# A layer with attention, retention and a gated MLP: the hand-written order at the start of the up projection ends earlier, and GpSimd's sums for the third column unit are tied there

## The chip, the cores and the metric

The kernel runs on one core of one Trainium2 chip. The metric is device time in microseconds (us) of one execution. TensorE (PE) multiplies, VectorE (DVE), ScalarE (ACT) and GpSimd (POOL) do the elementwise work, and SyncE (SP) issues most of the DMAs. Each engine runs its own list of instructions in order and waits where an instruction needs something that another engine or a DMA has not yet delivered.

## The reference

One layer of a diffusion backbone over 1024 latent tokens of width 1024, in fp32. An attention and a retention branch are merged and added to `x`; the change lies behind all that, where the MLP begins:

```python
hx2 = _modulate(_rmsnorm(x, norm2_g[l]), sh2, sc2)
x = x + g2 * _conv_ffn(hx2, w_up[l], conv_w[l], conv_b[l], w_down[l])
...
def _conv_ffn(h, w_up, conv_w, conv_b, w_down):
    u = h @ w_up                                   # (1024 x 1024) @ (1024 x 5632)
    n = u.shape[1]
    pad = CONV_W // 2
    up = jnp.pad(u, ((0, 0), (pad, pad), (0, 0)))
    u = sum(up[:, i:i + n] * conv_w[i] for i in range(CONV_W)) + conv_b
    a, val = jnp.split(u, 2, axis=-1)
    return (jax.nn.silu(a) * val) @ w_down
```

`D_FF` is 2816, so `u` has 5632 columns; `CONV_W` is 3 and runs along the tokens.

## The kernel before, in words

**Precision.** A product of fp32 matrices is made of three passes over operands that are split in a high and a low part (`split`, L86 and L87): ScalarE casts the block to fp32r (the high half), and VectorE subtracts that from the block (the low half). `open3` issues high x high, high x low and low x high as `PE L1374`. A weight tile is `wc` in the profile; the raw blocks that it is split from are `ur` (loaded), `s` (summed) or `raw`.

**The up projection.** The columns of `w_up` are worked off in units: a unit holds one block of gate columns and the block of value columns that goes with it, and computes `u` for both and all tokens, as a 2 x 2 product by seven multiplications in place of eight. The weight's quarters are a11, a12, a21, a22, and four sums of them s1 to s4; the moving side has the quarters B11, B21, B22 and four differences of quarters, the "combinations" T1 to T4. The seven products are a11·B11, s2·T2, s1·T1, s3·T3, a12·B21, a22·T4 and s4·B22, each of twelve 128x512 matmuls. The class `Seven` holds the general form: `load` reads the four raw quarters and makes s1 to s4 on GpSimd (L1388 to L1391), `prod` splits a weight and multiplies, `step` says what belongs to each product. The banks are named X, Y, Z and W; sums of banks on VectorE (`p1`, `u2`, `u3`, in tiles `pu`) give the four quarters of `u` (tiles `uu`), and `conv` (L1815 to L1840) makes the convolution and the gate of a finished unit.

**The start by hand.** The last token block, `LAST` (block 7 of 8), is still being normalized when the up projection begins. Two units, n = 0 and 1 (`EARLY` is 2), therefore begin early: their weight sums stand ready in memory (`us`, from `d_u`), and each product of theirs is issued as soon as the part of the moving side that it needs is there. The order of this stretch is written out by hand in a block `with tc.manual_schedule():` (L1924 to L2006). Within it, every engine gets its instructions in the order of the code. Outside of it a scheduler sets each engine's order at build time. The functions of the stretch:

- `copy_p1(n)` copies the first product of unit n out of its bank on ScalarE (L1796), so that a12·B21 may be added into the same bank.
- `norm_rows(LAST, g)` writes the normalized rows of the last block, on ScalarE (L1714, `h2h`, and L1716, `vr`) and VectorE; `norm_comb` (L1725) makes the last block's part of a combination. Its results stand in `vo` and `vr`.
- `comb_raw(c, b)` loads block b of combination c+1 from the scratch `d_t` (tile `tr`, on SP's queue, L1781). `comb_split(c, b, t)` splits it into the tiles of T1 to T4. Blocks 0 to 2 come from the scratch, block 3 is the last token block's.
- `close(0)`, `close(1)` and `close(2)` of a unit make its products with T2, T3 and T4 and VectorE's sums with them. In `close(0)` of before, the parameters `first` and `last` cut the work of unit 1 in two: `first=False` issues the product alone, `last=False` the sums alone.
- `units[2].load(with_vec)` loads the quarters of unit 2, the first that is not early. `with_vec` ties the first of its four GpSimd sums to the last VectorE instruction written before it:

```python
def with_vec(ins):
    prev = next(i for i in reversed(nc.cur_bb.bb.instructions) if i.engine == mybir.EngineType.DVE)
    tc.add_manual_dep(ins.ins, prev.name, mybir.DependencyInfo(mybir.DependencyClass.Sync, mybir.DependencyReason.DATA))
```

In before that instruction is the convolution's L1824 of unit 0, since `units[0].close(2)`, which completes unit 0, is the last line of the block. Behind the block the loop over `interleaved(EARLY, NF)` makes the steps of all further units, in the scheduler's order.

Of the kernel before, what the change touches and what calls it, by code (L numbers as in the profile page):

```python
# [8 lines left out]
F32 = mybir.dt.float32  # L9
# [7 lines left out]
P = 128  # L17
# [15 lines left out]
NF = FF // P  # L33
# [7 lines left out]
def tile_hybrid_layer(ctx, tc: tile.TileContext, io, dbg=None):  # L41
    nc = tc.nc
    vec, act, pool, pe, sync = nc.vector, nc.scalar, nc.gpsimd, nc.tensor, nc.sync
# [265 lines left out]
    first = [[wtile() for _ in range(2)] for _ in range(3)]  # L309
# [702 lines left out]
    us = []  # L1012
# [274 lines left out]
    mix, last = None, (None, None)  # L1287
    for h in range(RH):
        head = Head(h)
        for i in range(NCB + NTB):  # L1290
# [3 lines left out]
            last = (head, i)  # L1294
# [336 lines left out]
    EARLY = 2  # L1631
# [132 lines left out]
    def w_split(raw):  # L1764
        w = wtile()
        split(w[:, 0], w[:, 1], raw)
        return w
# [11 lines left out]
    def comb_raw(c, b):  # L1779
        t = gtile(0, F32, "tr")  # L1780
        sync.dma_start(t, d_t[c, b])  # L1781
        return t

    def comb_split(c, b, t):
        split(combs[f"T{c + 1}"][0][:, b], combs[f"T{c + 1}"][1][:, b], t if len(t.shape) == 3 else t.rearrange("p (k t) -> p k t", k=KH))
# [8 lines left out]
    def copy_p1(n):  # L1794
        p1e.append(gtile(0, F32, "pu"))
        act.copy(p1e[n], early[n][0][:, 0:512])  # L1796
# [48 lines left out]
    class Up(Seven):  # L1845
# [19 lines left out]
            self.p1, self.W = p1e[self.n], early[self.n][1][:, 512:1024]  # L1865
            self.c11()

        def close(self, n, first=True, last=True):
            if n == 0:
                if first and last or not first:  # L1870
                    self.u2, self.u3 = (self.tmp() for _ in range(2))
                    self.prod(self.Y, us[self.n, 1], "T2", True, False)
                if not first:
                    return
                vec.tensor_tensor(self.u2, self.Y, self.p1, ALU.add)
                vec.tensor_tensor(self.u2, self.W, self.u2, ALU.add)
                self.add(0, 1, self.Z, self.u2)
            elif n == 1:
                self.prod(self.Y, us[self.n, 2], "T3", False, False)
                vec.tensor_tensor(self.u3, self.Y, self.p1, ALU.add)  # L1880
                self.add(1, 1, self.Z, self.u3)
            else:
                self.prod(self.Y, a22[self.n], "T4", False, True)
                self.add(1, 0, self.Y, self.p1)
# [31 lines left out]
    with tc.manual_schedule():  # L1916
        out_begin(LAST)
        ra = [up_raw(n, 0, 0) for n in range(EARLY)]
        norm_begin(LAST - 1)
        norm_begin(LAST)  # L1920
        out_mm(LAST, 0)
        wu[0, "a11"], wu[1, "a11"] = w_split(ra[0]), w_split(ra[1])
        out_add(LAST, 0)
        out_mm(LAST, 1, range(0, KH))  # L1924
        norm_turn(LAST - 1, 1)
        norm_turn(LAST - 1, 0)
        out_mm(LAST, 1, range(KH, KB))
        ra = [up_raw(n, 0, 1) for n in range(EARLY)]
        tr = {(0, b): comb_raw(0, b) for b in range(2)}
        norm_rows(LAST - 1, 1)  # L1930
        norm_rows(LAST - 1, 0)
        early.append(early_bank(0))
        mm_seven(early[0][0][:, 0:512], wu[0, "a11"], h2_rows(0, 0), True, False)
        out_add(LAST, 1)
        norm_square(LAST)
        po.release()
        pu.append(ps("u_ps1", "left"))
        wop.release()
        gpool[1].release()
        rp = sb("raws", "right")  # L1940
        tpl = sb("combs", "right")
        us = {(n, 3): ur_load(d_u[n, 3]) for n in range(EARLY)}
        for c in ("T1", "T2", "T3", "T4"):
            combs[c] = [tpl.tile([P, 4, KH, P], F32R, name=f"{c}{i}") for i in range(2)]
        sync.dma_start(d_x1[LAST * P : NTB * P], tok[LAST]["x"])
        cs = {c: norm_comb(LAST - 1, c) for c in (0, 2)}
        norm_scale(LAST)
        cs.update({c: norm_comb(LAST - 1, c) for c in (1, 3)})
        wu[0, "a12"] = w_split(ra[0])
        wu[1, "a12"] = w_split(ra[1])  # L1950
        early.append(early_bank(1))
        mm_seven(early[1][0][:, 0:512], wu[1, "a11"], h2_rows(0, 0), True, False)
        norm_turn(LAST, 1, early[0][1][:, 0:512])
        norm_turn(LAST, 0, early[1][1][:, 0:512])
        copy_p1(0)
        for c in range(4):
            store_comb(LAST - 1, c, cs[c])
        us.update({(n, c): ur_load(d_u[n, c]) for c in (0, 1, 2) for n in range(EARLY)})
        a22 = [ur_load(units[n].src[1, 1]) for n in range(EARLY)]
        op.release()  # L1960
        tap = sb("conv", "right")
        mm_seven(early[0][0][:, 0:512], wu[0, "a12"], h2_rows(KH, 0), False, True)
        wu[0, "s4"] = w_split(us[0, 3])
        norm_rows(LAST, 1)
        copy_p1(1)
        mm_seven(early[1][0][:, 0:512], wu[1, "a12"], h2_rows(KH, 0), False, True)
        norm_rows(LAST, 0)
        tr[0, 2] = comb_raw(0, 2)
        mm_seven(early[0][1][:, 512:1024], wu[0, "s4"], h2_rows(KH, 1), True, True)
        wu[1, "s4"] = w_split(us[1, 3])  # L1970
        mm_seven(early[1][1][:, 512:1024], wu[1, "s4"], h2_rows(KH, 1), True, True)
        for b in range(2):
            comb_split(0, b, tr[0, b])
        t0 = norm_comb(LAST, 0)
        wu[0, "s1"] = w_split(us[0, 0])
        comb_split(0, 2, tr[0, 2])
        comb_split(0, 3, t0)
        mm_seven(early[0][1][:, 0:512], wu[0, "s1"], comb_rows("T1"), True, True)
        tr.update({(c, b): comb_raw(c, b) for c in (1, 2) for b in range(3)})
        wu[1, "s1"] = w_split(us[1, 0])  # L1980
        t2 = norm_comb(LAST, 2)
        t1 = norm_comb(LAST, 1)
        mm_seven(early[1][1][:, 0:512], wu[1, "s1"], comb_rows("T1"), True, True)
        units[0].open()
        units[1].open()
        comb_split(1, 3, t1)
        for b in range(3):
            comb_split(1, b, tr[1, b])
        t3 = norm_comb(LAST, 3)
        units[0].close(0)  # L1990
        units[1].close(0, first=False)
        comb_split(2, 3, t2)
        for b in range(3):
            comb_split(2, b, tr[2, b])
        units[1].close(0, last=False)
        units[0].close(1)
        tr.update({(3, b): comb_raw(3, b) for b in range(3)})
        cw = tap.tile([P, 2 * NF, 3], F32, name="cw")
        sync.dma_start(cw, io["conv_w"])
        cb = tap.tile([P, 2 * NF], F32, name="cb")  # L2000
        sync.dma_start(cb, io["conv_b"])
        comb_split(3, 3, t3)
        for b in range(3):
            comb_split(3, b, tr[3, b])
        units[1].close(1)
        units[0].close(2)  # L2006
    units[2].load(with_vec)
    units[2].step(0)
    units[1].close(2)
    for i, n in interleaved(EARLY, NF):  # L2010
# [239 lines left out]
```

## Time and profile before

| | |
|---|---|
| time, median of 3 runs | 1794.78 us (1793.72 to 1796.03) |
| the profiled execution | 1792.47 us, of which the span of its instructions 1790.7 |
| TensorE busy | 1724.9 us, 96%, 8333 matmuls |
| VectorE busy | 1322.9 us, 74% |
| ScalarE busy | 853.9 us, 48% |
| GpSimd busy | 585.0 us, 33% |
| DMA | 265.28 MB, mean 148 GB/s |
| granted TensorE clock, mean | 0.985 |

Busy shares are averages over the whole span. Of the forty equal slices of the span (44.8 us each), TensorE is at nine tenths or more in all but five; two of the five, with seven and six tenths, are the slices from 1119 to 1209 us, and the granted clock there is eight tenths. The hand-written stretch at the start of the up projection lies there.

### The profile page before, as it was taken

Reading aid. Unit: us, or ns where it says so; the run is one execution under the profiler, and the core shown is the slowest. Engines: PE = TensorE matmul, PEld = TensorE weight load, DVE = VectorE, ACT = ScalarE, POOL = GpSimd, SP = SyncE. Lnnn points to the kernel's source line nnn. Section 1 sums busy time; section 2 is a strip of 40 time slices with the busy share of each in tenths; the row PEclk is TensorE's granted clock in tenths of the full one; section 3 lists DMA queues with packets and bytes.
Section 4 is the critical chain, followed back from the end, with each engine's and each line's share of the span. In section 5 each row is a group of like instructions: output and inputs, shape, how many; then the busy total and the mean of one; then the engine's idle time right before and its main releaser. Section 6 shows DMA issues by size and latency. Waiting matters only on the chain.

```text
span 1790.7 us, 24670 instructions
## 1 busy us (share of the span) xinstructions
PE 1724.9 (96%) x8333; PEld 1428.3 (80%) x8333; DVE 1322.9 (74%) x2444; ACT 853.9 (48%) x1843; POOL 585.0 (33%) x485
## 2 busy tenths in 40 slices
PE   7799999999999999999999999769999999999997
PEld 3588888888888888788888887658888888788886
DVE  4978888766776776866755577589889989876755
ACT  5667666553443444543443234444444444554444
POOL 2610000003334343565403221065555555211444
PEclk9899999999999999999999999889999999999999
DMA  8133334432231213577567557332332333486753
GB/s 341 56 123 120 108 115 138 130 120 96 75 103 42 72 42 118 169 247 241 178 233 268 198 200 255 118 112 88 99 108 88 103 120 101 165 285 196 236 170 147
DMA packets 142143, 265.28 MB, mean 148 GB/s; under 512 B 16160, under 2 KB 28608, under 8 KB 142016
## 3 DMA queue, kind: packets, MB, share of 16 engines
q1 hardware_dynamic: 121360, 234.86, 40.0%
q10 hardware_dynamic: 20656, 28.84, 4.4%
q8 instruction: 65, 1.06, 0.2%
q14 instruction: 62, 0.51, 0.1%
HBM read 190.49 MB, written 70.53 MB: 146 GB/s over the span
## 4 chain that ended last, share of the span: by engine, by line
PE 45%; issue 5%; DVE 4%; POOL 3%; ACT 1%; DMA 0%; POOLq 0%; DVEq 0%; ACTq 0%
PE u L1374 30%; PE y L1374 4%; PE pr L111 2%; PE pr L112 2%; PE pr L110 2%; PE om L123 2%; PE om L122 2%; PE om L121 2%; DVE wc L87 1%; POOL x L2064 1%; PE pn L112 1%; PE pn L110 1%; PE pn L111 1%; POOL pd L2101 0%; DVE at L1821 0%
## 5 line engine op out<-in xcount | busy, mean ns | idle before, releaser
L1374 PE MATMUL u<-T,wc 128*128 128x512 f32 x1056 | 256.9, 400 | 20.7 <-DVE wc L87 9.3
L1374 PEld LDWEIGHTS u<-T,wc 128*128 128x128 f32 x1056 | 201.9, 193 | 69.2 <-DVE wc L87 11.8
L1374 PE MATMUL y<-wc,ahl 128*128 128x512 f32 x924 | 212.3, 392 | 3.1 <-DVE wc L87 1.8
L1374 PEld LDWEIGHTS y<-wc,ahl 128*128 128x128 f32 x924 | 174.5, 189 | 40.5 <-DVE wc L87 2.5
L87 DVE TENSOR_TENSOR wc<-ur,wc 128x512 fp32r<-128x512 f32 x147 | 132.5, 905 | 64.3 <-ACT wc L86 64.3
L86 ACT CAST wc<-ur 128x512 fp32r<-128x512 f32 x147 | 90.9, 622 | 121.2 <-PE y L1374 72.1
L1374 PE MATMUL u<-h2a,wc 128*128 128x512 f32 x528 | 125.2, 392 | 5.7 <-DVE pu L1422 3.5
L111 PE MATMUL mm<-low,wc 128*128 128x512 f32 (+1 forms) x328 | 124.1, 378 | 0.0
L1374 PEld LDWEIGHTS u<-h2a,wc 128*128 128x128 f32 x528 | 98.9, 188 | 28.2 <-issue 3.4
L110 PE MATMUL mm<-hx,wc 128*128 128x512 f32 x264 | 107.6, 408 | 0.3 <-DVE vc L221 0.3
L112 PE MATMUL mm<-hx,wc 128*128 128x512 f32 x264 | 105.1, 398 | 0.0
L86 ACT CAST wc<-s 128x512 fp32r<-128x512 f32 x80 | 49.7, 622 | 93.8 <-PE u L1374 88.7
L1513 POOL TENSOR_TENSOR col<-col,bcol 128x32 f32<-128x32 f32 x1 | 0.2, 250 | 281.9 <-DVE aw L538 281.9
L123 PE MATMUL mm<-wc,low 128*128 128x512 f32 (+1 forms) x240 | 91.3, 381 | 0.0
L1374 PE MATMUL u<-hxT,wc 128*128 128x512 f32 x384 | 89.8, 390 | 0.0
L87 DVE TENSOR_TENSOR wc<-s,wc 128x512 fp32r<-128x512 f32 x80 | 88.3, 1105 | 0.3
L1374 PEld LDWEIGHTS u<-hxT,wc 128*128 128x128 f32 x384 | 72.0, 188 | 15.2 <-issue 0.3
L87 DVE TENSOR_TENSOR wc<-raw,wc 128x512 fp32r<-128x512 f32 x88 | 67.2, 774 | 21.1 <-ACT wc L86 20.9
L1388 POOL TENSOR_TENSOR s<-ur 128x512 f32<-128x512 f32 x20 | 33.8, 1690 | 143.6 <-DVE wc L87 68.1
L121 PE MATMUL mm<-wc,hx 128*128 128x512 f32 x192 | 75.3, 392 | 0.6 <-ACT r L1105 0.6
L122 PE MATMUL mm<-wc,hx 128*128 128x512 f32 x192 | 75.3, 392 | 0.0
L87 DVE TENSOR_TENSOR wc<-wr,wc 128x512 fp32r<-128x512 f32 x56 | 54.6, 979 | 23.1 <-ACT wc L86 22.9
(395 smaller groups left out, 4642.0 us busy)
## 6 DMA issues: line engine op xcount, KB each, us to landing
ur<-in_w_up SPq DMA_DIRECT2D x82, 256.0 KB, 2.8
ur<-d_a SPq DMA_DIRECT2D x77, 256.0 KB, 3.0
aw<-in_w_ada SPq DMA_DIRECT2D x32, 512.0 KB, 3.3
pj<-in_w_down SPq DMA_DIRECT2D x44, 256.0 KB, 4.7
d_w<-pj SPq DMA_DIRECT2D x44, 256.0 KB, 2.0
d_a<-sa SPq DMA_DIRECT2D x44, 256.0 KB, 2.0
ur<-d_w SPq DMA_DIRECT2D x44, 256.0 KB, 3.5
d_a<-at SPq DMA_DIRECT2D x33, 256.0 KB, 2.6
```

Source lines behind the costliest of these rows:

```text
L86: act.copy(hi, src)
L87: (lo_eng or vec).tensor_tensor(lo, src, hi.bitcast(F32), ALU.subtract)
L110: pe.matmul(out, wh, xh, start=k == 0, stop=False)
L111: pe.matmul(out, wh, xl, start=False, stop=False)
L112: pe.matmul(out, wl, xh, start=False, stop=k == n - 1)
L121: pe.matmul(out, ah, bh, start=first, stop=False)
L122: pe.matmul(out, ah, bl, start=False, stop=False)
L123: pe.matmul(out, al, bh, start=False, stop=last)
L1374: pe.matmul(out, a, b, start=first and n == 0, stop=last and n == 2, skip_group_check=True)
L1388: pin(pool.tensor_tensor(self.s1, self.a21, self.a22, ALU.add))
L1513: pool.tensor_tensor(col[:, 16:48], col[:, 16:48], bcol[:, 16:48], ALU.add)
L2064: pool.tensor_tensor(z, z, fg[:, gs(dh)], ALU.mult)
```

## The change

It has three parts. In the block, `copy_p1(1)` moves ahead of `norm_rows(LAST, 1)`. The block now ends behind `comb_split(2, 3, t2)`, which is the last token block's split of the third combination, T3; all that followed in it is outside, in the scheduler's hands, and `units[2].load(with_vec)` stands first there, so that the tie is to that split. The loads of T4's three blocks now stand with their splits, behind the loads of the convolution's constants `cw` and `cb`. And `close(0)` loses its two parameters.

```diff
-        def close(self, n, first=True, last=True):
+        def close(self, n):
             if n == 0:
-                if first and last or not first:
-                    self.u2, self.u3 = (self.tmp() for _ in range(2))
-                    self.prod(self.Y, us[self.n, 1], "T2", True, False)
-                if not first:
-                    return
+                self.u2, self.u3 = (self.tmp() for _ in range(2))
+                self.prod(self.Y, us[self.n, 1], "T2", True, False)
                 vec.tensor_tensor(self.u2, self.Y, self.p1, ALU.add)
...
         wu[0, "s4"] = w_split(us[0, 3])
+        copy_p1(1)
         norm_rows(LAST, 1)
-        copy_p1(1)
         mm_seven(early[1][0][:, 0:512], wu[1, "a12"], h2_rows(KH, 0), False, True)
...
         t3 = norm_comb(LAST, 3)
-        units[0].close(0)
-        units[1].close(0, first=False)
         comb_split(2, 3, t2)
-        for b in range(3):
-            comb_split(2, b, tr[2, b])
-        units[1].close(0, last=False)
-        units[0].close(1)
-        tr.update({(3, b): comb_raw(3, b) for b in range(3)})
-        cw = tap.tile([P, 2 * NF, 3], F32, name="cw")
-        sync.dma_start(cw, io["conv_w"])
-        cb = tap.tile([P, 2 * NF], F32, name="cb")
-        sync.dma_start(cb, io["conv_b"])
-        comb_split(3, 3, t3)
-        for b in range(3):
-            comb_split(3, b, tr[3, b])
-        units[1].close(1)
-        units[0].close(2)
     units[2].load(with_vec)
+    for n in range(EARLY):
+        units[n].close(0)
+    for b in range(3):
+        comb_split(2, b, tr[2, b])
+    cw = tap.tile([P, 2 * NF, 3], F32, name="cw")
+    sync.dma_start(cw, io["conv_w"])
+    cb = tap.tile([P, 2 * NF], F32, name="cb")
+    sync.dma_start(cb, io["conv_b"])
+    comb_split(3, 3, t3)
+    for b in range(3):
+        comb_split(3, b, comb_raw(3, b))
+    units[0].close(1)
+    units[1].close(1)
+    units[0].close(2)
     units[2].step(0)
     units[1].close(2)
```

ScalarE, at the copy. `pu` from `u_11964` is the copy of unit 1's first product, `h2h` are the last block's rows, `wc_12024` is the high half of a weight of unit 0. Before:

```order
L1796 COPY pu_11986<-u_11908 128x512
L86 CAST wc_12024<-ur_11938 128x512
L1714 ACTIVATE h2h_11647<-u_11909,col_83,a2_8902 128x128
L1714 ACTIVATE h2h_11649<-u_11909,col_83,a2_8902 128x128
L1714 ACTIVATE h2h_11651<-u_11909,col_83,a2_8902 128x128
L1714 ACTIVATE h2h_11653<-u_11909,col_83,a2_8902 128x128
L1796 COPY pu_12039<-u_11964 128x512
```

And now:

```order
L1796 COPY pu_11986<-u_11908 128x512
L86 CAST wc_12024<-ur_11938 128x512
L1796 COPY pu_12027<-u_11964 128x512
L1714 ACTIVATE h2h_11647<-u_11909,col_83,a2_8902 128x128
L1714 ACTIVATE h2h_11649<-u_11909,col_83,a2_8902 128x128
L1714 ACTIVATE h2h_11651<-u_11909,col_83,a2_8902 128x128
L1714 ACTIVATE h2h_11653<-u_11909,col_83,a2_8902 128x128
```

The copy of unit 1 has moved ahead of the four activations; they and what follows stand one place later.

VectorE, from the second combination's last splits on. `T21`, `T31` and `T41` are the low halves of T2, T3 and T4; `wc` from `ur_11996` and `ur_11998` are the low halves of s2 of unit 0 and 1, of `ur_12000` that of s3 of unit 0; L1875 and L1876 (in the new kernel L1872 and L1873) are the sums `u2` of unit 0, L1403 the sum that goes to `uu`. Before:

```order
L87 TENSOR_TENSOR T21_11945<-tr_12114,T20_11944 128x512
L1725 TENSOR_TENSOR vo_11813<-vo_11813,vr_11811 128x512
L87 TENSOR_TENSOR wc_12156<-ur_11996,wc_12156 128x512
L1875 TENSOR_TENSOR pu_12154<-u_11908,pu_11986 128x512
L1876 TENSOR_TENSOR pu_12154<-u_11909,pu_12154 128x512
L1403 TENSOR_TENSOR uu_12139<-u_11909,pu_12154 128x512
L87 TENSOR_TENSOR wc_12176<-ur_11998,wc_12176 128x512
L87 TENSOR_TENSOR T31_11947<-vr_11810,T30_11946 128x512
L87 TENSOR_TENSOR T31_11947<-tr_12116,T30_11946 128x512
L87 TENSOR_TENSOR T31_11947<-tr_12118,T30_11946 128x512
L87 TENSOR_TENSOR T31_11947<-tr_12120,T30_11946 128x512
L1875 TENSOR_TENSOR pu_12174<-u_11964,pu_12039 128x512
```

And now, where the low halves of both units' s2, from `ur_11996` and `ur_11998`, stand directly ahead of T2's four splits, the last of which is the first row here:

```order
L87 TENSOR_TENSOR T21_11945<-tr_12114,T20_11944 128x512
L1725 TENSOR_TENSOR vo_11813<-vo_11813,vr_11811 128x512
L87 TENSOR_TENSOR T31_11947<-vr_11810,T30_11946 128x512
L87 TENSOR_TENSOR T31_11947<-tr_12116,T30_11946 128x512
L87 TENSOR_TENSOR T41_11949<-vo_11813,T40_11948 128x512
L87 TENSOR_TENSOR T31_11947<-tr_12118,T30_11946 128x512
L1872 TENSOR_TENSOR pu_12173<-u_11908,pu_11986 128x512
L87 TENSOR_TENSOR T31_11947<-tr_12120,T30_11946 128x512
L1873 TENSOR_TENSOR pu_12173<-u_11909,pu_12173 128x512
L87 TENSOR_TENSOR wc_12237<-ur_12000,wc_12237 128x512
```

Both weights' low halves have moved ahead of T2's four splits, T3's splits ahead of most of the sums, and the split that the GpSimd sum is tied to is the row `T31<-vr`.

SP's queue, from T3's blocks on. `tr` from `d_t` are blocks of T3 (`tr_12116` to `tr_12120`) and then of T4, `ur` from `in_w_up` the raw quarters of unit 3. Before:

```order
L1781 DMA tr_12116<-d_t_66 128x512
L1781 DMA tr_12118<-d_t_66 128x512
L1781 DMA tr_12120<-d_t_66 128x512
L1781 DMA tr_12219<-d_t_66 128x512
L1781 DMA tr_12221<-d_t_66 128x512
L1781 DMA tr_12223<-d_t_66 128x512
L1999 DMA cw_12225<-in_conv_w 128x132
L2001 DMA cb_12227<-in_conv_b 128x44
L1827 DMA d_a_64<-at_12270 128x512
L1789 DMA ur_12409<-in_w_up 128x512
```

And now:

```order
L1781 DMA tr_12116<-d_t_66 128x512
L1994 DMA cw_12219<-in_conv_w 128x132
L1996 DMA cb_12221<-in_conv_b 128x44
L1781 DMA tr_12118<-d_t_66 128x512
L1781 DMA tr_12120<-d_t_66 128x512
L1789 DMA ur_12409<-in_w_up 128x512
L1789 DMA ur_12411<-in_w_up 128x512
L1781 DMA tr_12225<-d_t_66 128x512
L1781 DMA tr_12229<-d_t_66 128x512
L1781 DMA tr_12233<-d_t_66 128x512
```

The constants have moved up, two raw quarters of unit 3 stand ahead of T4's blocks, and the store of unit 0's convolution (L1827) behind them.

## The prediction

> **What bounds the kernel now.** I read the page first: TensorE is busy nearly all the time and holds most of the chain that ended last, so a gain has to come from stretches where it waits.
>
> ```profile
> span 1790.7 us, 24670 instructions
> PE 1724.9 (96%) x8333; PEld 1428.3 (80%) x8333; DVE 1322.9 (74%) x2444; ACT 853.9 (48%) x1843; POOL 585.0 (33%) x485
> PE 45%; issue 5%; DVE 4%; POOL 3%; ACT 1%; DMA 0%; POOLq 0%; DVEq 0%; ACTq 0%
> ```
>
> Then I cut the place of the change into windows. Columns: stretch, its length, busy time and instructions of PE, weight loads, DVE, ACT, POOL, then granted clock, DMA share, GB/s.
>
> ```profile
> 1120.12:1128.42 8.30, 8.30 (x37) 6.87 (x37) 6.03 (x11) 6.05 (x13) 0.00 (x0) 1.00 0.93 317
> 1128.42:1137.20 8.78, 8.77 (x39) 6.95 (x37) 4.71 (x8) 6.61 (x12) 0.00 (x0) 1.00 0.53 171
> 1137.20:1168.40 31.20, 22.57 (x70) 17.12 (x70) 18.41 (x28) 7.04 (x11) 0.00 (x0) 0.78 0.09 28
> 1168.40:1199.52 31.12, 16.48 (x61) 12.10 (x61) 30.80 (x22) 11.79 (x16) 26.69 (x15) 0.84 0.38 127
> 1199.52:1215.84 16.32, 16.32 (x73) 13.52 (x72) 12.83 (x13) 6.71 (x9) 7.53 (x6) 1.00 0.21 64
> 1215.84:1235.00 19.16, 19.16 (x86) 15.88 (x85) 16.24 (x18) 8.78 (x12) 7.23 (x5) 1.00 0.23 69
> ```
>
> From 1137 to 1199.5 TensorE loses time twice over, by waits and by a lower clock. Ahead and behind it is full, and behind it stays full through the rest of the up projection, so what is won by 1216 should be kept. In the second half of the hole VectorE is full (30.80 of 31.12) while in the first it is busy 18.41 of 31.20 and GpSimd not at all: work that could run early runs late. The timeline of TensorE names the waits (start, length, operation, count, idle before and releaser):
>
> ```profile
> 1115.75 2.57 PE L1374 MATMUL u<-h2a,wc 128*128 128x512 f32 x10 [0.37 <-DVE wc L87]
> 1120.12 3.02 PE L1374 MATMUL u<-h2a,wc 128*128 128x512 f32 x12 [1.80 <-ACT pu L1796]
> 1128.42 8.78 PE L1374 MATMUL u<-T,wc 128*128 128x512 f32 x38
> 1139.58 4.59 PE L1374 MATMUL u<-T,wc 128*128 128x512 f32 x12 [2.38 <-DVE wc L87]
> 1146.44 4.61 PE L1374 MATMUL u<-T,wc 128*128 128x512 f32 x12 [2.27 <-DVE wc L87]
> 1155.03 5.49 PE L1374 MATMUL u<-T,wc 128*128 128x512 f32 x12 [3.98 <-DVE wc L87]
> 1177.60 5.39 PE L1374 MATMUL u<-T,wc 128*128 128x512 f32 x14 [9.15 <-ACT wc L86]
> 1213.12 5.60 PE L1374 MATMUL u<-h2a,wc 128*128 128x512 f32 x24
> ```
>
> One matmul takes (8.78-0.39)/37 = 0.227 us at full speed, a product of twelve 2.72. Three waits are for the low half of a weight that stands on VectorE behind sums of the product before: the two engines wait in turn. VectorE's side of it, every wait from 1128 to 1214.9 (waiter, releaser: us in total, times, longest):
>
> ```profile
> DVE pu L1880 <- PE u L1374: 7.7, 2, 4.2
> DVE pu L1875 <- PE u L1374: 5.0, 2, 3.3
> DVE uu L1403 <- PE u L1374: 4.5, 2, 3.1
> DVE wc L87 <- ACT wc L86: 1.5, 1, 1.5
> DVE T L87 <- ACT T L86: 0.7, 1, 0.7
> DVE at L1821 <- ACT at L1820: 0.6, 1, 0.6
> DVE pu L1416 <- PE u L1374: 0.2, 1, 0.2
> ```
>
> They add up to 20.2 us. The same VectorE instructions stand in both kernels up to unit 3's u3 sum (L1422 at 1214.17 below), so this is also the most that VectorE can be earlier there, if its instructions cost the same.
>
> **The rows for the costs.** VectorE, GpSimd and ScalarE, then a transfer of a block from the scratch:
>
> ```profile
> 1126.31 0.68 DVE L87 TENSOR_TENSOR T<-vo,T 128x512 fp32r<-128x512 f32 x1
> 1128.23 0.69 DVE L1725 TENSOR_TENSOR vr<-vr,vo 128x512 f32<-128x512 f32 x1
> 1140.04 1.89 DVE L87 TENSOR_TENSOR T<-tr,T 128x512 fp32r<-128x512 f32 x3
> 1177.90 1.76 DVE L87 TENSOR_TENSOR wc<-s,wc 128x512 fp32r<-128x512 f32 x1
> 1187.43 0.68 DVE L1416 TENSOR_TENSOR pu<-u,pu 128x512 f32<-128x512 f32 x1
> 1214.17 0.68 DVE L1422 TENSOR_TENSOR pu<-u,pu 128x512 f32<-128x512 f32 x1
> 1172.52 2.18 POOL L1388 TENSOR_TENSOR s<-ur 128x512 f32<-128x512 f32 x1 [59.54 <-DVE at L1824]
> 1200.45 1.29 POOL L1391 TENSOR_TENSOR s<-ur,s 128x512 f32<-128x512 f32 x1
> 1113.51 0.62 ACT L86 CAST wc<-ur 128x512 fp32r<-128x512 f32 x1
> 1119.49 0.58 ACT L1796 COPY pu<-u 128x512 f32<-128x512 f32 x1
> 1125.05 0.62 ACT L86 CAST T<-tr 128x512 fp32r<-128x512 f32 x1 [1.50 <-DMA tr<-d_t]
> DMA to landing us min/median/max: 2.7/3.3/6.6
> ```
>
> A split's low half alone is 0.69, one after another (1.89-0.69)/2 = 0.60. Beside a GpSimd sum it is 1.76, and the sum 2.18 instead of 1.29. A VectorE operation that reads PSUM keeps 0.68 beside GpSimd (1187.43).
>
> The Trainium skill, "SBUF — State Buffer", section "Who interferes with whom", says that a VectorE instruction with two SBUF inputs contends with a GpSimd instruction that reads SBUF and that the loser fully blocks. That only such operations suffer agrees with the 0.68. By a full block a split would take 1.29 + 0.69 = 1.98, and four of them 0.9 us more than below, so the gain would be 15.4 instead of 16.3; the row has 1.76, and I use that.
>
> **The copy of unit 1's first product.** It ran at 1119.49 behind four activations, and TensorE waited 1.80 for it. In the new order it follows the cast of 1113.51 and ends near 1114.7, so the product starts at 1115.75 + 10 x 0.227 = 1118.02, 2.10 earlier; the activations pushed back by at most 0.5 wait for VectorE anyway. The next stop eats part: the first combination's last block lands at 1125.05 and its low half ends at 1126.99 (row 1126.31), so S1 begins at about 1126.8 instead of 1128.42, and S1 and S2 together end 48 x 0.227 later, at 1137.7. I cost this part at 0: what it leaves is covered by the wait for T3 below. Without that cover it would be worth 1.6.
>
> **The second combination's products.** Both weights' splits now stand ahead of the combination's, so the pair runs without a stop and the wait of 2.38 goes. Late next is T3. VectorE from 1128.83: two weight halves, four of T2, one difference, the first of T3 are eight of 0.60; the eighth ends at 1128.83 + 7 x 0.60 + 0.69 = 1133.72. GpSimd's sums of unit 2, tied to that one, start there and not at 1172.5.
>
> **T3 under the sums.** Behind stand three SBUF splits at 1.70 (to 1138.8), the PSUM sum of unit 0 (0.60), T3's last split (1.70, 1141.1), a second sum (0.7) and the weight's low half (0.6): T3 of unit 0 can run at 1142.4. TensorE has waited 4.7 since 1137.7. Bounds: with no contention 4 x 1.1 = 4.4 earlier; with the four sums at 2.2 each holding the splits throughout, 3.3 later.
>
> **The clock.** After the waits the granted clock drops (columns: stretch, length, PE busy, clock, DMA):
>
> ```profile
> 1138.00:1140.00 2.00, 0.42 (x2) 1.00 0.00 0
> 1140.00:1142.00 2.00, 2.00 (x7) 0.57 0.24 67
> 1144.00:1146.00 2.00, 0.17 (x1) 1.00 0.31 94
> 1148.00:1150.00 2.00, 2.00 (x6) 0.50 0.00 0
> ```
>
> A wait of 2.38 was followed by half speed, which ended some 3.4 us later although TensorE then worked slowly: full work at half speed releases it. I take one such stretch for T3: ten matmuls at 0.454 end at 1147.0. VectorE comes to its next wait four operations after 1142.3, at 1144.7, and loses 2.3. At full speed it loses nothing; with a second stretch 1.7 more goes.
>
> The Trainium skill, "TensorE: Matmul & The Clock Gate", section "The HAM clock gate (the "warmup" mystery)", gives half clock only after an idle window of about 3.4 us. These rows show it after 2.38, so the measurement decides; if by the rule neither new wait halved the clock, the gain would be 16.3 + 2.3 + 1.7 = 20.3.
>
> **The fourth combination.** Its three loads now stand on SP's queue behind unit 3's first two raw weights, which wait for GpSimd's third sum and for T3's weight split (1142.4). They issue at 1143 to 1144.3 and land near 1147.6; on ScalarE their casts stand behind unit 2's s1 cast, which waits for the product ending at 1147.0, and end at 1149.2. VectorE has three sums until 1148.8 and then the three splits, so it does not wait; a landing of 6.6 would cost it up to 3.3. The conv constants go ahead on SP by some 0.8 us and delay nothing.
>
> **To the common point.** From 1147 VectorE has the same work as before and no product that it must wait for; I allow 0.9 for small waits. So 20.2 - 2.3 - 0.9 = 17.0 earlier at L1422 of unit 3, 1197.2. TensorE would be ready for unit 3's A12 product 190 matmuls (43.1) after 1142.4, plus 2.3 for half speed and about 6 for single low halves, at 1194: VectorE bounds, as between 1168 and 1199 before. The product follows at once, where before it came at 1213.12 + 12 x 0.227 = 1215.84, 1.0 after the sum's end: +1.0. The wait of some 3 to 4 costs one half-speed stretch: -1.7. Behind that point the orders are equal again on all engines but for single rows. Sum: 17.0 + 1.0 - 1.7 = 16.3 us. The profiled execution is 1792.47 (span 1790.7 and 1.8 around it) and would be 1776.2; the median of the runs is 1794.78, and I set the gain against that: 1778.5.
>
> **The rivals.**
> More: contention is less, and TensorE, not VectorE, sets the pace. Without the VectorE waits left (20.2) or the half speed, with the 1.0, and with the four sums at 0.9 less each, 20.2 + 1.0 + 3.6 = 24.8, 1770.0. For it: the PSUM operations between the splits are free of it. Against: 30.80 of 31.12.
> Less: the sums run at 2.2 each (3.3 late), the fourth combination's loads land after 6.6 (3.3), and T3 and T4 each get one more half-speed stretch (3.4): 16.3 - 10 = 6.3, 1788.5. The full DMA share of 0.93 ahead of 1128 speaks for slow landings, the 0.09 after 1137 against.
> Slower: the clock. If single-product waits hold half speed from T3 to unit 3's A12, 192 matmuls take 87 us from 1142.4 and end at 1229.5 instead of 1215.84: 1808.5. It decides once some 131 of the 192 run at half speed, since (73.4-43.6)/0.227 = 131. Against it: fully busy half speed ended after one stretch at 1144.
> Same: the early sums win what VectorE, already full at 1168, gives back in waits, 1794.8. Against it: the 15.9 us that VectorE waits before 1166 are in the 20.2.
>
> **Chances.** Likeliest, a gain of 12 to 21: 0.60. More: 0.12. Less, 4 to 12: 0.18. Same: 0.05. Slower: 0.05. A measurement of this kernel tells about 0.2%, 3.6 us, from no change: faster 0.90, same 0.05, slower 0.05. The range of 1770.0 to 1788.5 holds the likeliest and most of its two neighbours.
>
> **What would show it.** Right: GpSimd's four sums begin within 2 us of 1133.7; no wait between the S2 products; one wait of 3 to 6 before T3 with half speed behind; splits near 1.7 beside the sums; VectorE full from 1147 to about 1197; the wait of 9.15 for the s cast gone; a wait for unit 3's L1422; the same distance from there to the end. Wrong: the sums later, a wait above 3 for the fourth combination, half speed over several stretches, or new waits behind 1200.

## The result, and the profile after

The changed kernel takes 1775.94 us, median of 4 runs (1775.07 to 1777.53), against 1795.4 of the kernel before: 19.5 us less, a ratio of 0.9894 with a 95% interval of 0.9877 to 0.9911. Forecast were 1778.5 us, a gain of 16.3, in a range of 1770.0 to 1788.5. Timed again in a later round, in five runs, the ratio was 0.9897 (0.9883 to 0.9911).

The profiled execution took 1775.89 us with a span of 1774.0. Its page begins:

```profile
span 1774.0 us, 24676 instructions
PE 1725.3 (97%) x8333; PEld 1427.3 (80%) x8333; DVE 1318.6 (74%) x2444; ACT 853.6 (48%) x1843; POOL 581.5 (33%) x485
PE 43%; issue 5%; DVE 4%; POOL 3%; ACT 1%; DMA 1%; SPq 0%; POOLq 0%; ACTq 0%; DVEq 0%
```

TensorE's share of the chain fell from 45% to 43%. Its busy time over the whole span is what it was, though it falls at the place of the change, as windows further below show. Before two traces are laid beside each other, their starts have to be made equal. The last token block's transposes (L1703) are ahead of everything that the change touches, and the first matmul of the down projection (`y`) is far behind it. TensorE's timeline has them in before:

```profile
1113.82 1.09 PE L1703 MATMUL u<-ident,xn 128*128 128x128 f32 x8 [0.62 <-DVE xn L1680]
...
1558.19 1.52 PE L1374 MATMUL y<-wc,ahl 128*128 128x512 f32 x6
```

And after:

```profile
1116.82 1.09 PE L1703 MATMUL u<-ident,xn 128*128 128x128 f32 x8 [0.61 <-DVE xn L1680]
...
1542.22 1.52 PE L1374 MATMUL y<-wc,ahl 128*128 128x512 f32 x6
```

The transposes come 3.00 us later after the change, though nothing ahead of them differs. 2.0 of that arise at the start of the program (the same L493 matmul starts at 195.69 in before's trace and at 197.69 in this one), and 0.9 more between 920 and 946 us. From the transposes to the down projection it is 444.37 us before and 425.40 after, so 18.97 less. I call this distance the stage; all differences below are taken from the transposes on.

The windows over the place of the change, moved by the 3.00 us against those of the prediction (columns as there: stretch, length, busy time and count of PE, weight loads, DVE, ACT, POOL, granted clock, DMA share, GB/s):

```profile
1131.42:1140.20 8.78, 8.78 (x41) 7.26 (x40) 8.29 (x12) 7.48 (x15) 3.46 (x3) 1.00 0.48 170
1140.20:1171.40 31.20, 25.47 (x101) 18.48 (x100) 30.78 (x36) 13.98 (x18) 10.16 (x6) 0.98 0.32 102
1171.40:1202.52 31.12, 27.33 (x110) 22.14 (x109) 29.18 (x27) 11.14 (x17) 20.09 (x12) 0.91 0.24 86
```

From 1140.2 to 1171.4 TensorE now gets 101 matmuls done where it did 70, at 0.98 of the full clock where 0.78 was granted; VectorE is busy 30.78 of 31.20 instead of 18.41, and GpSimd has six sums there instead of none. TensorE's timeline shows which waits are left:

```profile
1118.74 5.28 PE L1374 MATMUL u<-h2a,wc 128*128 128x512 f32 x22 [0.36 <-DVE wc L87]
...
1129.85 10.95 PE L1374 MATMUL u<-T,wc 128*128 128x512 f32 x47 [0.16 <-DVE T L87]
1141.29 0.47 PE L1374 MATMUL u<-T,wc 128*128 128x512 f32 x1 [0.50 <-DVE pu L1872]
1142.28 0.50 PE L1374 MATMUL u<-T,wc 128*128 128x512 f32 x1 [0.52 <-DVE T L87]
1143.97 5.29 PE L1374 MATMUL u<-T,wc 128*128 128x512 f32 x22 [1.18 <-DVE wc L87]
...
1169.35 4.62 PE L1374 MATMUL u<-T,wc 128*128 128x512 f32 x12 [2.88 <-DVE pu L1416]
...
1197.95 4.39 PE L1374 MATMUL u<-h2a,wc 128*128 128x512 f32 x12 [3.79 <-DVE pu L1422]
1202.18 8.35 PE L1374 MATMUL u<-T,wc 128*128 128x512 f32 x36
```

The copy's wait of 1.80 is gone, S1 and S2 run through, T3 waits three times but 2.20 in all, and the waits of 9.15 and of 2.27 to 3.98 are gone. Two waits for VectorE's sums are left behind, with half speed behind each (4.62 and 4.39 for twelve matmuls that take 2.72). GpSimd's timeline, and VectorE's rows beside its sums:

```profile
1136.67 1.63 POOL L1388 TENSOR_TENSOR s<-ur 128x512 f32<-128x512 f32 x1 [20.69 <-DMA tr<-d_t]
1138.37 1.62 POOL L1389 TENSOR_TENSOR s<-s,ur 128x512 f32<-128x512 f32 x1
1139.96 1.72 POOL L1390 TENSOR_TENSOR s<-ur 128x512 f32<-128x512 f32 x1
1141.64 1.72 POOL L1391 TENSOR_TENSOR s<-ur,s 128x512 f32<-128x512 f32 x1
...
1137.63 1.21 DVE L87 TENSOR_TENSOR T<-vo,T 128x512 fp32r<-128x512 f32 x1 [0.49 <-ACT T L86]
1138.77 1.78 DVE L87 TENSOR_TENSOR T<-tr,T 128x512 fp32r<-128x512 f32 x1
1140.47 0.68 DVE L1872 TENSOR_TENSOR pu<-u,pu 128x512 f32<-128x512 f32 x1
1141.07 1.16 DVE L87 TENSOR_TENSOR T<-tr,T 128x512 fp32r<-128x512 f32 x1
1142.76 1.16 DVE L87 TENSOR_TENSOR wc<-ur,wc 128x512 fp32r<-128x512 f32 x1
```

The sums begin at 1136.67. The block that the row names as releaser had landed at 1135.39; the split of the tie ended at 1136.53, so it is the tie. The first split shown (`T<-vo`) is T4's, the next two are T3's. The splits beside them take 1.16 to 1.78 instead of 0.6 to 0.7, and the sum that reads PSUM keeps its 0.68.

### The profile page after: what moved, and what is told of

Read it like the earlier page. It is cut to its first block, busy times and chain, and to the rows that moved or that the text cites. A ratio compares the mean times of both kernels' runs of the same rounds, so it can differ in the third digit from the quotient of the medians.

```text
span 1774.0 us, 24676 instructions
## 1 busy us (share of the span) xinstructions
PE 1725.3 (97%) x8333; PEld 1427.3 (80%) x8333; DVE 1318.6 (74%) x2444; ACT 853.6 (48%) x1843; POOL 581.5 (33%) x485
## 4 chain that ended last, share of the span: by engine, by line
PE 43%; issue 5%; DVE 4%; POOL 3%; ACT 1%; DMA 1%; SPq 0%; POOLq 0%; ACTq 0%; DVEq 0%
PE u L1374 28%; PE y L1374 4%; PE pr L111 2%; PE pr L110 2%; PE pr L112 2%; PE om L121 2%; PE om L122 2%; PE om L123 2%; DVE wc L87 1%; DMA tr<-d_t 1%; POOL x L2059 1%; PE pn L112 1%; PE pn L111 1%; PE pn L110 1%; DVE at L1821 0%
## 5 line engine op out<-in xcount | busy, mean ns | idle before, releaser
L1374 PE MATMUL u<-T,wc 128*128 128x512 f32 x1056 | 251.8, 393 | 6.0 <-DVE pu L1416 2.9
L1374 PEld LDWEIGHTS u<-T,wc 128*128 128x128 f32 x1056 | 198.0, 189 | 53.7 <-ACT pu L1413 3.4
L86 ACT CAST wc<-s 128x512 fp32r<-128x512 f32 x80 | 49.7, 621 | 88.2 <-PE u L1374 85.4
```

What stands on the lines that cost most here:

```text
L86: act.copy(hi, src)
L1374: pe.matmul(out, a, b, start=first and n == 0, stop=last and n == 2, skip_group_check=True)
```

## The experiments

Each run is told with its ratio to the kernel before (95% interval) and its stage. Two traces of one kernel gave stages of 444.4 and 444.3 (before), 429.4 and 429.4 (the changed kernel with late sums), and 425.4 and 428.2 (the changed kernel). That the first two pairs agree so well is partly luck: in before's second trace TensorE came to unit 2's product behind L1422 1.6 us sooner after the transposes (81.25 against 82.89) and lost the 1.6 again to half speed behind it.

| kernel | ratio (95%) | median us | stage us |
|---|---|---|---|
| before | 1 | 1793.3 to 1796.1 | 444.4, 444.3 |
| the change | 0.9894 (0.9877 to 0.9911), 0.9897 (0.9883 to 0.9911) | 1775.94, 1774.76 | 425.4, 428.2 |
| copy alone | 0.9988 (0.9976 to 0.9999) | 1791.29 | 443.3 |
| change without the copy | 0.9899 (0.9881 to 0.9916) | 1775.00 | 427.7 |
| early sums alone | 0.9935 (0.9918 to 0.9953) | 1781.66 | 432.6 |
| change with late sums | 0.9903 (0.9885 to 0.9921) | 1775.68 | 429.4, 429.4 |
| sums behind T3 | 0.9868 (0.9855 to 0.9882) | 1770.55 | 421.0 |
| T4's loads early | 0.9884 (0.9868 to 0.9899) | 1772.69 | 424.5 |
| sums behind T3, T4's loads early, convolutions late | 0.9864 (0.9847 to 0.9880) | 1769.45 | 419.7 |
| sums behind T3, convolutions late | 0.9856 (0.9837 to 0.9876) | 1769.29 | 421.8 |

**The copy alone**, on the kernel before:

```diff
+        copy_p1(1)
         norm_rows(LAST, 1)
-        copy_p1(1)
```

> Before, with the copy of unit 1's first product ahead of the four activations and nothing else. Theory (the copy frees TensorE 1.6 to 2.1 earlier, and in the old order nothing covers it, since the sums of each product wait for that product and all that follows moves with them): 1.6 to 2.1 us faster than before, 1793.3 to 1793.8 against 1795.4. Rival (a later wait takes it, as it would in the changed kernel): within 0.5 of before. Rival (other waits fall on other moments of the clock gate): more than 3 either way.

The stage is 1.1 us shorter, and the ratio allows 0.2 to 4.3 us; the medians differ by 2.0. TensorE's timeline shows where the 2.1 went:

```profile
1125.90 0.50 PE L1374 MATMUL u<-T,wc 128*128 128x512 f32 x1 [0.55 <-ACT T L86]
1126.70 5.96 PE L1374 MATMUL u<-T,wc 128*128 128x512 f32 x25 [0.30 <-DVE T L87]
1133.02 3.02 PE L1374 MATMUL u<-T,wc 128*128 128x512 f32 x12 [0.35 <-DVE wc L87]
```

The product starts 2.1 sooner, but waits for T1's last block and for a weight follow, and the last matmul of these rows, the second of unit 1's S2, ends at 1136.04, 23.34 after the transposes (1112.70 here), against 23.38 before. So at that place the gain is zero, by my first rival; the 1.1 that is left arises behind it. There the clock falls differently: twelve matmuls from unit 0's T3 on took 3.01 behind its wait of 1.98, where before they took 4.61 behind 2.27, and unit 2's product behind L1422 took 4.39 instead of 2.97. Whether the copy alone is worth anything stays open.

**The change without the copy**, its counterpart (in the changed kernel, `copy_p1(1)` back behind `norm_rows(LAST, 1)`):

> The changed kernel with the copy at its old place, behind the four activations; the scheduler may order what follows the block otherwise. Theory (covered: the changed kernel waits 0.50 + 0.52 + 1.18 = 2.2 us ahead of and in T3's first product for VectorE, so TensorE 1.6 to 2.1 later there costs nothing): the changed kernel's time within 0.8, 1775.1 to 1776.7. Rival (not covered): 1.6 to 2.1 slower than the changed kernel, 1777.5 to 1778.0.

With 1775.00 us it is as fast as the change. S2 ends 25.63 after the transposes, 1.65 later than in the change's trace (23.98), and unit 1's T3 ends 33.33 after them, 0.89 later (32.44). The cover takes 0.8 of 1.65 there, and the stage of 427.7 lies between the change's two. What follows can't be compared row by row, since the scheduler orders the rest differently there.

**The early sums alone**, on the kernel before, inside its block:

```diff
         comb_split(2, 3, t2)
+        units[2].load(with_vec)
...
         units[0].close(2)
-    units[2].load(with_vec)
```

> Before, with the load of unit 2 and the tie of its first GpSimd sum behind the last token block's split of T3, inside the old block; the order of products, splits and sums of units 0 and 1 stays as it was. Theory (the larger part of the gain is the 15.9 us in which VectorE and TensorE wait for each other in turn, and these stay; the sums then run in VectorE's waits, so that the four VectorE instructions beside them from 1173.6 to 1181.8 lose their excess of 0.9 to 1.1 each, 4.0 in all, and three to five splits of 0.6 to 0.7 fill waits): 6 to 8 us faster than before, 1787.4 to 1789.4. Rival (the early sums are the bulk of it): 14 or more faster, 1781 or less. Rival (the waits in turn set the pace whatever GpSimd does): within 2 of before.

It gained 0.65%, 11.6 us, and 11.8 in the stage: more than I allowed, less than the rival. The waits in turn are still there, 2.38 and 2.40 in TensorE's row; what went is the wait of 9.15 for the cast of a sum: between the T2 products and unit 3's L1422 no wait above 2.66 is left. I had counted the splits that fill VectorE's waits, but not that TensorE's longest wait of the stretch hung on GpSimd. By VectorE's rows up to unit 3's L1422, it waited 7.1 us less (13.6 against 20.7), and its slow rows lost 3.2 less beside GpSimd, where 4.0 was forecast.

**The change with late sums**, the other half:

```diff
-    units[2].load(with_vec)
     for n in range(EARLY):
         units[n].close(0)
...
     units[0].close(2)
+    units[2].load(with_vec)
     units[2].step(0)
```

> The changed kernel with the load of unit 2 back at its old place, so that its first GpSimd sum is tied to the convolution of unit 0 as before; copy and new order of products stay. Theory (the waits in turn are gone, 15.9 of VectorE's 20.2 less what T3 costs, but GpSimd's sums again start behind the convolution and run beside VectorE when it is full): 11 to 14 us faster than before, 1781.4 to 1784.4, and TensorE again waits several us for the cast of a weight sum. Rival (without early sums the wait moves from VectorE to that cast): 0 to 5 faster, 1790.4 or more. Rival (the tie is worth nothing, the order all): the changed kernel's time within 1.5, 1774.4 to 1777.4.

By its time of 1775.68 it would be the last rival: the tie is worth nothing. By the stage it is 15.0 shorter than before, just above the 11 to 14 of the theory, and 4.0 or 1.2 longer than the change. In the two traces the execution with late sums came to its transposes 5.2 us sooner (1111.64 against 1116.82), so that differences of a few us can only be read by the stage. TensorE's timeline:

```profile
1124.89 16.58 PE L1374 MATMUL u<-T,wc 128*128 128x512 f32 x71 [0.31 <-DVE T L87]
...
1160.42 5.86 PE L1374 MATMUL u<-T,wc 128*128 128x512 f32 x14 [9.32 <-ACT wc L86]
```

S1, S2 and T3 of both units now run in one piece behind a wait of 0.31, and T3 ends 29.8 us after the transposes, against 32.4 in the change. The early sums therefore cost T3 2.6 us through VectorE's slower splits; late, they cost the wait of 9.32 behind. The kernel with late sums once more:

> The changed kernel with late sums once more, for its stage, which was 429.4 against 425.4 and 428.2 of the changed kernel. Theory (the tie as it stands in the change is worth 1 to 4 us of the 19): 428 to 431. Rival (it is worth nothing, or costs as much in T3's splits as it brings behind): 424 to 427.5.

The stage was 429.4 again, although the transposes came at 1118.26 this time, 6.6 us later than in the first trace (the one execution took 1781.56 us). By the stage the tie as the change has it is worth 1.2 to 4.0 of the 19; by the times of the runs it cannot be told from nothing. VectorE's L1422 of unit 3, which comes ahead of the half speed behind it, is a clearer mark. In the change, then with late sums:

```profile
1197.13 0.68 DVE L1422 TENSOR_TENSOR pu<-u,pu 128x512 f32<-128x512 f32 x1
```

```profile
1197.00 0.68 DVE L1422 TENSOR_TENSOR pu<-u,pu 128x512 f32<-128x512 f32 x1
```

That is 80.3 us after the transposes in the change (81.4 in its second trace) and 85.4 with late sums (85.4 again), so the tie brings VectorE there 4.0 to 5.1 sooner. Behind it the change loses 1.0 to 2.9 of this to a wait of 3.79 and half speed. The parts overlap: 11.8 and 15.0 are more than 19.0, since early sums and the new order fill the same waits. The kernel before, once more:

> The kernel before once more, for its stage alone: 444.4 in the trace shown. Two runs of the changed kernel gave 425.4 and 428.2. If the same holds here, 442 to 447.

It gave 444.3, in one execution of 1789.62 us.

**The sums behind T3**, tied to the last of its splits instead of the first:

```diff
-    units[2].load(with_vec)
     for n in range(EARLY):
         units[n].close(0)
     for b in range(3):
         comb_split(2, b, tr[2, b])
+    units[2].load(with_vec)
```

> The changed kernel with the load of unit 2 behind the three splits of T3's loaded blocks, so that its first GpSimd sum is tied to T3's last split instead of its first; VectorE's order is the same for the next ten instructions. Measured by the stage from the last token block's transposes to the down projection's first matmul, which is 444.4 us in before, 425.4 in the changed kernel and 429.4 with late sums. Theory (the early sums slow T3's own splits, since with late sums the T3 products follow without a wait and end 2.6 us earlier after the transposes; sums that begin 4 to 5 later are still in time for their casts): stage 422 to 424, no wait above 0.5 ahead of T3. Rival (VectorE is the bound up to unit 3 and the sums only slow other splits): 424.7 to 426. Rival (the sums come late for the casts): 427 or more.

The stage is 421.0, and the time 1770.55 against 1774.76 of the changed kernel on the same chip. The rows that were slow before, on VectorE, then the sum and TensorE's T3:

```profile
1137.03 0.69 DVE L87 TENSOR_TENSOR T<-vo,T 128x512 fp32r<-128x512 f32 x1
1137.64 0.69 DVE L87 TENSOR_TENSOR T<-tr,T 128x512 fp32r<-128x512 f32 x1
1138.84 0.68 DVE L87 TENSOR_TENSOR T<-tr,T 128x512 fp32r<-128x512 f32 x1
...
1139.66 1.29 POOL L1388 TENSOR_TENSOR s<-ur 128x512 f32<-128x512 f32 x1 [24.43 <-DVE T L87]
...
1141.55 5.29 PE L1374 MATMUL u<-T,wc 128*128 128x512 f32 x22 [0.48 <-DVE wc L87]
```

The same instructions at 0.68 and 0.69, one wait of 0.48, and the sums are still in time. That is the theory, and the stage is 1.0 below its window. VectorE comes to unit 3's L1422 76.4 us after the transposes (1116.07 here), 3.9 and 5.0 sooner than in the change's two traces:

```profile
1192.46 0.68 DVE L1422 TENSOR_TENSOR pu<-u,pu 128x512 f32<-128x512 f32 x1
```

Up to there its slow rows lose 11.7 us beside GpSimd instead of 14.6, and it waits 1.5 instead of 2.9. The counterpart, the changed kernel on that chip, was this:

> The changed kernel once more, so that the three others stand beside it on the same chip. Stage 425.4 within 0.8 (the trace shown) and 19 us less than before; if the stage differs by more than 1 between two runs of the same kernel, differences of that size say nothing.

Its stage was 2.8 longer than in the first trace, a miss. The profiled execution was the slowest of its five (1779.79). Behind the same wait of 3.79 its twelve matmuls took 5.46 instead of 4.39, and the next 36 took 8.79 instead of 8.35, 1.5 in all; 0.8 more was lost ahead of S1, which began 13.26 after the transposes instead of 12.48. So a difference of one pair of stages below 3 us says nothing here.

**T4's loads early:**

```diff
         comb_split(2, 3, t2)
+        tr.update({(3, b): comb_raw(3, b) for b in range(3)})
...
-        comb_split(3, b, comb_raw(3, b))
+        comb_split(3, b, tr[3, b])
```

> The changed kernel with T4's three loads inside the block, ahead of unit 3's raw weights on SP's queue. The scheduler then puts T4's splits ahead of the low half of s3 of unit 0, so that T3's first product has to wait for seven more VectorE instructions of 0.6 us, 4.2 in all. Theory (VectorE sets the pace up to unit 3, and TensorE makes the time good in its later waits of 2.9 and 3.8 us): stage 424 to 426.5, as in the changed kernel's 425.4, with a wait of 4 to 7 ahead of T3. Rival (TensorE sets the pace): 4 to 6 slower, 429.4 to 431.4. Rival (the loads were late in the changed kernel and cost more than its waits of 0.19 and 0.23 show): 423 or less.

```profile
1140.91 0.73 PE L1374 MATMUL u<-T,wc 128*128 128x512 f32 x2 [2.38 <-DVE pu L1872]
1143.91 9.71 PE L1374 MATMUL u<-T,wc 128*128 128x512 f32 x32 [2.27 <-DVE wc L87]
```

TensorE waits 0.49, 0.53, 2.38 and 2.27, 5.7 us ahead of and in T3 instead of 2.2, and the stage is 424.5, in the theory's window. The mechanism is another, though. VectorE from L1725 to unit 3's L1422:

```profile
1126.77:1192.06 65.29, 55.26 (x228) 43.51 (x227) 58.40 (x66) 30.36 (x45) 29.26 (x18) 0.95 0.34 112
```

VectorE was idle 6.9 us in that stretch, against 2.9 in the change, and its slow rows lost only 10.9 beside GpSimd, against 14.6. Besides, one convolution row of unit 2 comes behind unit 3's L1422 here and not ahead of it. That these cancel is luck, and TensorE had no wait left for that L1422. So this run does not show that VectorE sets the pace. Whether the loads themselves gain (1772.69 against 1774.76) is within the intervals.

**The convolutions late.** In the code the call of `conv` for unit 0 stands ahead of unit 2's product with T2 (the two texts below say behind it), and the call for unit 1 ahead of its product with B21, first with both edits above:

```diff
+                if self.n < EARLY:
+                    held.append(self)
+                else:
+                    conv(self.j, *self.u)
...
     for i, n in interleaved(EARLY, NF):
+        if (i, n) in ((2, 1), (2, 4)):
+            u = held.pop(0)
+            conv(u.j, *u.u)
```

> A trial of a better order: the changed kernel with both edits above, and with the convolutions of units 0 and 1 written behind unit 2's product with T2 and ahead of its product with B21, so that the scheduler gives the sums that TensorE waits for the first place on VectorE. Theory (the changed kernel's two late waits, 2.88 for unit 2's L1416 and 3.79 for unit 3's L1422, and the half speed behind them, 1.9 and 1.5, come from convolution instructions ahead of these sums, and behind unit 3 VectorE has room for them): 3 to 7 us faster than the same kernel without the convolutions moved, stage 416 to 421. Rival (the work on VectorE is the same and it is the bound, so that the wait only moves): 422 to 426.

The stage of 419.7 lies in the theory's window, but only 1.3 below the kernel with the sums behind T3 alone, and two edits differ. So I ran it with one:

> The kernel with sums tied to T3's last split (stage 421.0) with one further edit: the convolutions of units 0 and 1 are written behind unit 2's product with T2 and ahead of its product with B21; T4's loads stay where the change puts them. Theory (the waits of 2.19 for L1416 and 2.57 for L1422 left in that kernel come from convolution instructions ahead of these two sums, and VectorE has room behind unit 3): stage 416.5 to 419, both waits below 1.5. Rival (VectorE has the same work and is the bound, so the wait moves to another place): 420 to 423.5, as two runs of the changed kernel lay 2.8 apart.

```profile
1158.26 3.02 PE L1374 MATMUL u<-T,wc 128*128 128x512 f32 x12 [1.52 <-DVE pu L1416]
...
1187.30 5.46 PE L1374 MATMUL u<-h2a,wc 128*128 128x512 f32 x12 [3.90 <-DVE pu L1422]
```

421.8: the wait for L1416 fell from 2.19 to 1.52, and the wait for unit 3's L1422 rose from 2.57 to 3.90. VectorE came to that L1422 76.0 us after the transposes, against 76.4 without the edit, so the outcome is the rival's. The theory was hardly tested, though: ahead of unit 2's L1416 VectorE still has the same five convolution rows (L1821 to L1824), only one row fewer stands ahead of unit 2's L1422, and the convolution ahead of unit 3's L1422 is unit 2's own, which the edit leaves where it was. All three kernels with the sums behind T3, at 1769.29 to 1770.55 us, beat the kernel before and the change; between them nothing is decided.

## Why the prediction was right, and by how much it was off

The chain of causes held, and most places fell on the forecast, once the 3.00 us of the later start are taken off.

- **The copy.** The product was to start at 1118.02: 1118.74 + 10 x 0.227 - 3.00 = 1118.01. S1 was to begin at 1126.8 and S2 to end at 1137.7; measured 1126.85 (its second matmul) and 1137.80. Cost 0 by cover: the run without the copy was as fast, within its interval.
- **The tie.** The sums were to start at 1133.72; 1136.67 - 3.00 = 1133.67.
- **T3 under the sums** was mis-sized. Forecast were four splits at 1.70, a wait of 4.7 and T3 at 1142.4; T4's first split, two of T3's and the weight's low half took 1.21, 1.78, 1.16 and 1.16 (excess over 0.68: 2.6 instead of 4.4), the waits were 2.20, and T3's main group ran at 1140.97. I had taken one row, 1.76 beside a sum, for all; a sum of PSUM stands between these splits, and each had to wait only for the rest of the GpSimd sum that was running. The prediction put the full block aside because 1.76 is less than 1.98. That reading was wrong: the split of that row began 1.04 us after its sum (1177.90 and 1176.86) and ended 0.55 after the sum's end, as a full block would have it (last section).
- **The clock at T3.** Forecast was one half-speed stretch that costs VectorE 2.3. Behind the shorter waits none came: 22 matmuls in 5.29. The prediction's other half-speed stretch, behind unit 3's L1422, came: 4.23 from 1197.95 to 1202.18 instead of 2.72, 1.5 lost of the 1.7 forecast. A third one, behind unit 2's L1416 and its wait of 2.88, was not in the forecast; it held VectorE's L1422 of unit 2 up by 1.13.
- **T4's loads** were issued from 1144.37 (forecast 1146 to 1147.3 on this clock) and cost VectorE one wait of 0.16.
- **VectorE to the common point.** From L1725 (1128.23 before, 1131.03 after) to unit 3's L1422 (1214.17 and 1197.13):

```profile
1128.23:1214.17 85.94, 62.66 (x235) 48.48 (x234) 65.28 (x67) 32.15 (x47) 32.62 (x19) 0.86 0.27 87
```

```profile
1131.03:1197.13 66.10, 57.41 (x236) 44.45 (x234) 63.24 (x68) 30.81 (x46) 30.36 (x19) 0.97 0.33 112
```

The first line is of before, the second of after. The stretch is 19.84 shorter where 17.0 was forecast: idle time fell from 20.66 to 2.86, which is 17.80, and busy time by 2.04. So the terms "-2.3" for T3's half speed (0) and "-0.9" for small waits (2.86, with the 1.13) nearly cancel, which is luck. The fall of busy time was not in the sum at all. Only 0.6 of it is less contention: the excess of the slow rows over their time alone (0.68 for a split, 1.27 and 1.21 for the convolution's) adds up to 15.2 before and 14.6 after. Another 1.2 is overlap: a row that follows directly begins up to 0.09 before the one ahead ends, 3.5 us in all before and 4.7 after, when fewer rows start behind a wait. The step of L1422 to the product gave 0.85 of the 1.0 forecast. Together 19.84 + 0.85 - 1.5 = 19.2, beside the stage's 18.97.

- **The rivals.** "Slower" needed half speed to last; in no trace did it last, from S1 on, over more than one product and the start of the next. "Same" needed the early sums to give the gain back in waits; the waits that came are 2.88 and 3.79, for VectorE's sums, and they are less than what went. "Less" needed slow sums and late loads; neither came. "More" had 3.6 us less contention, of which 0.6 came, and TensorE setting the pace; in the change TensorE waits for VectorE's sum at unit 3, so VectorE sets it there.

## What to carry to other kernels

Where two engines wait for each other in turn, as here, the gain lay in putting the work that the other engine needs next ahead of the sums that wait for it; the new order and the early start of a third engine filled the same waits, so their gains did not add. An early start was better tied behind the last operand that the busy engine still had to make, not the first, because the two hold each other up: the tie moved by three splits was worth another 4 us here. For changes of this size compare a stage between two fixed instructions, because the time ahead of the change alone moved by 6.6 us between two executions of one kernel here. And look within the stage at where half speed fell: it hid 1.0 to 2.9 us of what the tie gains.

## What the hardware showed that I had not expected

The length of a wait does not decide whether half speed follows. TensorE's rows behind the waits for L1416 and L1422, in before:

```profile
1188.26 2.98 PE L1374 MATMUL u<-T,wc 128*128 128x512 f32 x12 [2.06 <-DVE pu L1416]
1196.71 2.97 PE L1374 MATMUL u<-h2a,wc 128*128 128x512 f32 x12 [2.76 <-DVE pu L1422]
```

In the second trace of the same kernel:

```profile
1194.23 4.59 PE L1374 MATMUL u<-h2a,wc 128*128 128x512 f32 x12 [2.74 <-DVE pu L1422]
```

In the change with late sums, first and second trace:

```profile
1171.07 4.58 PE L1374 MATMUL u<-T,wc 128*128 128x512 f32 x12 [2.06 <-DVE pu L1416]
```

```profile
1177.76 3.01 PE L1374 MATMUL u<-T,wc 128*128 128x512 f32 x12 [2.05 <-DVE pu L1416]
```

And with the early sums alone:

```profile
1205.10 3.00 PE L1374 MATMUL u<-h2a,wc 128*128 128x512 f32 x12 [3.35 <-DVE pu L1422]
```

After 2.06 and after 2.75 us the same kernel ran once at full and once at half speed, and after 3.35 it ran at full speed. What decides is how a wait lies on a grid. In every trace here the granted clock changes only at moments that are whole multiples of 3.41 us apart, and the grid begins at another moment in each execution; in before, for example, the clock falls to half at 1140.30, rises at 1143.71 and falls at 1147.13. These are the grid's windows in which the six waits above lie for the most part, in the same order (stretch, length, PE busy and count, granted clock, DMA share, GB/s):

```profile
1184.67:1188.08 3.41, 1.53 (x7) 1.00 0.05 13
1194.91:1198.33 3.42, 1.61 (x7) 1.00 0.93 270
1190.86:1194.27 3.41, 0.67 (x4) 1.00 0.61 204
1168.51:1171.92 3.41, 1.35 (x7) 1.00 0.42 140
1174.12:1177.54 3.42, 1.58 (x7) 1.00 0.16 39
1203.32:1206.73 3.41, 1.63 (x7) 1.00 0.00 0
```

Half speed followed the third and the fourth, in which TensorE was busy 0.67 and 1.35 us, and not the others, with 1.53 to 1.63. In the thirteen traces, from 1095 to 1725 us, all 28 windows at full clock with at most 1.36 us of work were followed by one at half speed, and no window with 1.53 or more was. The border is not exact: one window at 722 us with 1.58 was followed by half speed. A window at half speed was followed by another up to 2.75 us of work and by full speed from 2.89 on. That is the difference between the change's two traces behind unit 3's L1422: 3.00 us of work in the first, 2.75 in the second, and there a second half-speed window came. One such stretch costs 1.5 to 2.6 us, so it is a noise of that size in every comparison.

The Trainium skill, "TensorE: Matmul & The Clock Gate", section "The HAM clock gate (the "warmup" mystery)", says that the activity window is free-running and does not restart with the kernel. That agrees with the grid above. That half speed takes at least one idle window of about 3.4 us does not: a window with 1.36 us of work was enough here.

VectorE and GpSimd kept each other out for whole instructions. In the change's rows above, the sums end at 1138.30, 1139.99, 1141.68 and 1143.36, and the split beside each ends 0.54 to 0.56 later (1138.84, 1140.55, 1142.23 and 1143.92). Each next sum in turn ends 1.13 to 1.15 after the split that began ahead of it ended. Alone, splits follow each other every 0.60 and a sum takes 1.29. So each of the two waits until the other's instruction is done, and then takes little less than its time alone. All slow splits from 1134 to 1225 us, in before and after the change, end 0.55 after a sum, and all slow sums end 1.12 to 1.16 after a VectorE instruction. Operations that read PSUM are not held up (0.68). Added up, this cost VectorE 14.6 of its 66.1 us from L1725 to unit 3's L1422 in the change, while its waits cost 2.9.
